# A two-layer DeltaNet and attention network on one core: an output head moved ahead of the recurrence's last round, a bank of its own for the last 256 columns, and four decayed values of the first step on GpSimd

## The chip, the core and the metric

The kernel runs as one program on one core of a Trainium2 chip. The core has a matrix engine (TensorE, PE in the profile; PEld is its weight load), a vector engine (VectorE, DVE), a scalar engine (ScalarE, ACT), a general engine (GpSimd, POOL) and a sync engine (SyncE, SP) that here only issues DMA transfers. Each engine works through its own list of instructions in order and waits at an instruction until the semaphores that it names are set. Matrix results go to PSUM, whose space is handed out in banks; everything else on the chip lies in SBUF, and the large intermediate arrays go out to the chip's memory (HBM) and come back.

The metric is the device time of one execution in microseconds (us), as the median of several runs. A profiled execution has its own time beside it; its span, from the first to the last record of the trace, is a little shorter.

## What is computed

The network has 512 latent tokens and 256 context tokens of width 1024 and two layers. Each layer is a modulated normalisation, a mixer, a gate and a residual sum. The mixer of layer 0 is a gated DeltaNet that runs over the tokens in both directions, with 16 value heads of 128 and chunks of 64 tokens; that of layer 1 is attention with 8 query heads, 2 key heads and an axial rotation. A last normalisation gives the output. What the change touches are the recurrence of layer 0, the output projection behind it and the end of the last layer:

```python
def step(s, xs):                                   # one chunk of 64 tokens, one direction
    qk_i, qd_i, kd_i, u_i, w_i, gl_i = xs
    v_new = u_i - jnp.einsum('bhcd,bhde->bhce', w_i, s)
    o = jnp.einsum('bhcd,bhde->bhce', qd_i, s) + jnp.einsum('bhcs,bhse->bhce', qk_i, v_new)
    s = s * gl_i[..., None, None] + jnp.einsum('bhcd,bhce->bhde', kd_i, v_new)
    return s, o
...
def finish(o, z):
    o = rms_norm(jnp.transpose(o, (0, 2, 1, 3)), o_norm_g).astype(z.dtype)
    return (o.reshape(b, l, DN_VAL_DIM) * jax.nn.silu(z)) @ w_out
...
        h_lat = h_lat + gate[:, None] * y_lat          # in both layers
...
    return rms_norm(h_lat, final_norm_g)
```

The state `s` starts at zero with the context, and what the context leaves in it is the start of the latent tokens.

## The kernel before, in words

**The recurrence.** It runs as 12 steps of one chunk in each direction (steps 0 to 3 the context, 4 to 11 the latent tokens), each in four parts of four heads. A piece is numbered x = 4·step + part, so there are 48. The loop `for x in range(50)` works on three pieces at a time: `products(x)`, `solve(x-1)`, `update(x-2)`.

- `products(x)` multiplies the state by keys and queries on PE (`ks`, L1562), forms the right side `r` on DVE (L1565), scales the query part into the output `O` or into `o` on ACT (L1568), and multiplies the state by its decay on POOL (`S`, L1571). On the second visit of a chunk POOL adds `o` into `O` (L1574). In step 0 the state is zero: there are no products, and `solve` takes the values directly.
- `solve(x)` multiplies by the inverted triangular matrices on PE (L1588) into the first half of a pair of PSUM banks, `pr_all` for even x and `pq_all` for odd x; ACT copies the result to `vn` (L1590); then four multiplications by a decay per token give `vd` (L1600 on ACT; in step 0, parts 0 and 1, L1598 on DVE).
- `update(x)` multiplies by the masked query-key products on PE (L1614) into the second half of the same pair of banks, and `vd` by the keys into `su` (L1622). The output is then copied (step 0, ACT, L1626) or added into `O` (DVE, L1628), and the state is copied (step 0, L1634) or added (L1636) on DVE.

As the banks alternate, `solve(x)` can only start when the reader of `update(x-2)`, at L1626 or L1628, is done with the same banks. There is one `su`, two each of `ks`, `r`, `vn` and `vd`.

**The order of the work.** PE, DVE, ACT and POOL follow the order in which this part of the program is written. SP's transfers are placed by the scheduler.

**The output seam.** The output projection of layer 0 runs over 32 units: two groups of three token tiles, 16 heads each. For one unit `out_load` (L1656) and `gate_load` (L1665) fetch the weights and the gate z; `out_high` (L1673, ACT) and `out_low` (L1680, POOL) split the weights into two parts `woh` and `wol`; `out_scale` (L1692, ACT) normalises the head's output into `so`; `out_turn` (L1699, PE) transposes it into `pt`; `out_gated` (L1708, DVE, three products) multiplies by the gate; `out_cast` (L1715, ACT) and `out_rest` (L1721, DVE) split the result into `y0` and `y1`; and `out_product` (L1742, PE) multiplies. The first unit's steps are written into the last rounds of the recurrence: the scaling at x = 45 and 46, the transposes at 46, gate, cast and rest at 47, between `solve(46)` and `update(45)`, and the first product at 48.

**The end.** In the last layer the output projection goes tile by tile (four of 128 tokens). `out_chunk` (L2442) runs the 24 matmuls of one chunk of columns, `finish_part` (L2448 to L2450) applies the gate, adds the residual and squares; `finish_sum` (L2454, L2456) and `finish_norm` (L2462 to L2465) give the inverse root, `weighed` (L2508) multiplies by the final weights. The last tile has three chunks, `(0, 512), (512, 256), (768, 256)`; the last two lie in the two halves of one bank, `po`. Behind the last one, ACT scales the first 512 columns (L2525) and DVE the others (L2527), and `send` (L2471) stores each half of the columns from the queue of ACT and of SP. A tile is made of 64 tokens each from two ends of the sequence, so `send` stores two pieces of 64 rows.

Of the kernel before, what the change touches and what calls it, by code (L numbers as in the profile page):

```python
# [12 lines left out]
ALU = mybir.AluOpType  # L13
# [4 lines left out]
P = 128  # L18
# [68 lines left out]
def backbone(tc, a, out):  # L87
# [1416 lines left out]
    if True:  # L1504
# [72 lines left out]
        def solve(x):  # L1577

            s, p = divmod(x, 4)
            t, visit = where(s)  # L1580
            Tt = loads[s][3]
            r, = live[x]
            pr_ = prq[x % 2][:, :, 0:2]
            for i in range(2):
                for j in range(2):
                    for hf in range(2):
                        r0, o0 = hf * 64, (hf ^ j) * 64
                        T.matmul(pr_[o0:o0 + 64, j, i], Tt[r0:r0 + 64, 4 * p + 2 * j + i, :], r[r0:r0 + 64, 2 * j + i], start=True, stop=True)  # L1588
            vn = ch.tile([P, 4, P], F32, tag="vn", name=f"vn{x}", bufs=2)
            (V.tensor_copy if x == 0 else S.copy)(vn.rearrange("p (j i) d -> p j i d", j=2), pr_)  # L1590
            vd = None
            if s < 11:
                vd = ch.tile([P, 4, P], F32, tag="vd", name=f"vd{x}", bufs=2)
                for c in range(4):
                    h = 4 * p + c
                    el = (elX if c > 1 else elV)[:, visit, t, h:h + 1]
                    if s == 0 and p < 2:
                        V.tensor_scalar(vd[:, c], vn[:, c], el, None, ALU.mult)  # L1598
                    else:
                        S.activation(vd[:, c], vn[:, c], AF.Copy, scale=el)  # L1600
            live[x] = [vn, vd]
# [99 lines left out]
    def out_gated(n, js=ALL):  # L1701

        gi, h = units0[n]
        pt, z = turned[n], zs_[n]
        for j in js:
            t, off, st_ = GROUPS[gi][j]
            pj = pt[:, j].rearrange("p (a k) -> p a k", a=2)
            V.scalar_tensor_tensor(pj, pj, og, raw(z, off, [[st_, 2], [1, 64]]), ALU.mult, ALU.mult)  # L1708
# [44 lines left out]
    AB, C = (0, 1), (2,)  # L1753
    squares = [(t, h) for t in (1, 0, 5) for h in range(VH)]
    for x in range(50):
        if x < 48:
            products(x)
        if x == 45:
            out_scale(0, AB)
        if x == 46:  # L1760
            out_scale(0, C)
        if 0 <= x - 1 < 48:
            solve(x - 1)
        if x == 47:
            out_gated(0)
            out_cast(0)
            out_rest(0)
        if 0 <= x - 2 < 48:
            update(x - 2)
        if x == 45:  # L1770
            psU_c.__exit__(None, None, None)
            psV_c = tc.tile_pool(name="psV", bufs=2, space=PSUM, reuse_waits="tile")
            turning["p"] = psV_c.__enter__()
        if 14 <= x < 30 or x >= 35:
            for t, h in squares[:2]:
                square_o(t, h)
            del squares[:2]
        if x == 1:
            V.tensor_tensor(or2, rq, rq, ALU.mult)
        if 30 <= x < 42:  # L1780
            some(ctx_chain, (2, 4, 1, 1, 1, 1, 1, 1, 1, 1, 1, 99)[x - 30])
        if x in (43, 44, 45):
            some(chain, (3, 7, 99)[x - 43])
        if x in (28, 32, 36, 40):
            with tc.issue_after(mark[0]):
                (out_load if x < 36 else gate_load)((x - 28) // 4 % 2)
        if x in (44, 45):
            out_high(x - 44)
        if x == 46:
            out_low(0)  # L1790
            out_turn(0)
        if x == 47:
            out_low(1)
            out_load(2)
        if x == 48:
            out_scale(1)
            out_product(0, 0)
            out_turn(1)
# [632 lines left out]
    gated(15)  # L2431


    acc = [pg, acc1, [tr_tile(f"pso2{nh}").rearrange("p a b -> p (a b)") for nh in range(2)], [s_all[:, 1024:1536], po]]

    jks = [f2.tile([P, D], F32, tag="jko", name=f"jko{t}") for t in range(2)]
    CHUNKS = [((0, 512), (512, 512))] * 3 + [((0, 512), (512, 256), (768, 256))]

    def out_chunk(k, t, c0, n):
        cc_, (bank, b0) = slice(c0, c0 + n), divmod(c0, 512)  # L2440
        for x, (i, j) in enumerate(PASS):
            T.matmul(acc[t][bank][:, b0:b0 + n], yT[i][:, k, t * P:(t + 1) * P], wo[j][:, k, cc_], start=k == 0 and x == 0, stop=k == KT - 1 and x == 2)  # L2442

    def finish_part(t, i):
        c0, n = CHUNKS[t][i]
        c, (bank, b0) = slice(c0, c0 + n), divmod(c0, 512)
        jk = jks[t]
        V.tensor_tensor(jk[:, c], acc[t][bank][:, b0:b0 + n], gate1[:, 0, c], ALU.mult)  # L2448
        V.tensor_tensor(hs[t][:, c], hs[t][:, c], jk[:, c], ALU.add)
        S.activation(jk[:, c], hs[t][:, c], AF.Square, accum_out=ss[:, t, i:i + 1])  # L2450
# [15 lines left out]
        return y  # L2466

    def send(t, x, c, q):
        for hf in range(2):
            c_ = t if hf == 0 else 7 - t  # L2470
            q(out[0, c_ * 64:c_ * 64 + 64, c], x[hf * 64:hf * 64 + 64, c])  # L2471
# [99 lines left out]
```

## Time and profile before

| | us |
|---|---|
| median of 3 runs | 1148.21 (1148.09 to 1150.12) |
| profiled execution, its own time | 1148.87 |
| its span | 1147.0 |
| PE busy | 1108.2 (97%) |
| DVE busy | 787.8 (69%) |
| ACT busy | 749.1 (65%) |
| POOL busy | 600.9 (52%) |
| granted PE clock (mean) | 0.995 |

The stages on the span's clock: the recurrence's first pieces start near 538, its step 1 near 548; from there to 709 it runs on; the seam lies between 709 and 718; the output projection fills the time to about 835; the last tile's matmuls end at 1136.2 and the last store is issued near 1142.8.

In the lines of the profile, L1588 is line 1588 of the kernel, `pr_all<-r,cT` names the tile written and those read, `128x512 f32` is partitions by elements, and `x16` the number of instructions in the row. In a timeline the first two numbers are start and duration in us, and the brackets hold the engine's idle time ahead of the row and what ended it. A row with several instructions gives the time from the first start to the last end. Matmuls are pipelined, so that consecutive rows of PE overlap a little.

### The profile page before, as it was taken

What the parts mean: (1) busy time and instruction counts of PE and PEld (TensorE: products, weight loads), DVE (VectorE), ACT (ScalarE), POOL (GpSimd) and SP (SyncE); (2) the same over time, 40 slices, a digit from 0 to 9 for tenths busy, and PEclk for the clock granted to TensorE, in tenths of its full rate; (3) what the DMA queues carried; (4) which work ended last, traced back from release to release, by engine and by line L of the source; (5) the groups of instructions that cost most, each with busy time, mean ns of one, the idle gap of its engine ahead of it and who ended that gap; (6) DMA issues with size and microseconds to landing.
All of it is one profiled execution on the core that took longest, in us unless ns stands there. A gap on an engine that the chain in (4) does not pass through costs nothing.

```text
span 1147.0 us, 27235 instructions
## 1 busy us (share of the span) xinstructions
PE 1108.2 (97%) x10511; PEld 904.6 (79%) x10511; DVE 787.8 (69%) x1628; ACT 749.1 (65%) x1998; POOL 600.9 (52%) x521
## 2 busy tenths in 40 slices
PE   5999999999999999998999999999999999999996
PEld 2777788888888888887566665888787889999885
DVE  4786656688899978783688877355546476667646
ACT  4554554477877888675789888875767356666731
POOL 0554111239999999940675688556645253130900
PEclk9999999999999999999999999999999999999999
DMA  9589744765748886756998983686844112001323
GB/s 367 199 287 326 261 143 130 226 178 166 232 128 241 264 246 205 207 181 193 291 258 244 276 252 101 196 224 184 239 136 138 55 57 63 30 19 56 111 74 92
DMA packets 117138, 208.69 MB, mean 182 GB/s; under 512 B 12145, under 2 KB 76818, under 8 KB 111762
## 3 DMA queue, kind: packets, MB, share of 16 engines
q1 hardware_dynamic: 97074, 195.32, 55.2%
q10 hardware_dynamic: 19936, 11.64, 3.4%
q8 instruction: 83, 1.36, 0.5%
q14 instruction: 45, 0.37, 0.1%
HBM read 166.16 MB, written 40.67 MB: 180 GB/s over the span
## 4 chain that ended last, share of the span: by engine, by line
PE 89%; DVE 3%; issue 2%; DMA 2%; ACT 2%; POOL 1%; SPq 0%; POOLq 0%; ACTq 0%; DVEq 0%
PE g_v L926 12%; PE g_z L926 12%; PE po L1742 9%; PE ks L1562 7%; PE g_k L500 6%; PE g_q L926 6%; PE pg L2162 4%; PE su L1622 3%; PE pg L2213 3%; PE po L2282 3%; PE s L2233 3%; PE kv L2044 2%; PE pa L316 2%; PE pt L2261 2%; PE pq_all L1588 1%
## 5 line engine op out<-in xcount | busy, mean ns | idle before, releaser
L1742 PE MATMUL po<-woh,y 128*128 128x512 f32 x384 | 129.2, 401 | 0.0
L1571 POOL TENSOR_TENSOR S<-S,glb 128x512 f32<-128x512 f32 x80 | 81.9, 1045 | 82.3 <-PE ks L1562 82.1
L1680 POOL TENSOR_TENSOR wol<-wo,woh 128x1024 fp32r<-128x1024 f32 x32 | 77.5, 2422 | 55.9 <-ACT woh L1673 54.2
L810 POOL TENSOR_TENSOR X<-X,tmp 128x62 f32<-128x62 f32 (+15 forms) x93 | 98.6, 1060 | 7.3
L809 POOL TENSOR_TENSOR tmp<-L,X 128x62 f32<-128x62 f32 (+15 forms) x93 | 91.9, 989 | 6.7
L926 PE MATMUL g_z<-uh,wh_z 128*128 128x512 f32 (+1 forms) x256 | 88.6, 346 | 0.0
L926 PE MATMUL g_v<-uh,wh_v 128*128 128x512 f32 (+1 forms) x256 | 88.0, 344 | 0.0
L941 DVE SCALAR_TENSOR_TENSOR acc_v<-g_v,cwv,acc_v 128x510 f32<-128x510 f32 (+3 forms) x128 | 77.7, 614 | 14.5 <-ACT acc_v L933 11.0
L926 PE MATMUL g_z<-ul,wh_z 128*128 128x512 f32 (+1 forms) x256 | 86.9, 339 | 0.4 <-issue 0.4
L926 PE MATMUL g_z<-uh,wl_z 128*128 128x512 f32 (+1 forms) x256 | 86.6, 338 | 0.0
L926 PE MATMUL g_v<-ul,wh_v 128*128 128x512 f32 (+1 forms) x256 | 86.1, 336 | 0.0
L926 PE MATMUL g_v<-uh,wl_v 128*128 128x512 f32 (+1 forms) x256 | 86.1, 336 | 0.0
L1742 PEld LDWEIGHTS po<-woh,y 128*128 128x128 f32 x384 | 72.3, 188 | 15.4 <-issue 0.3
L1742 PE MATMUL po<-wol,y 128*128 128x512 f32 x192 | 75.4, 393 | 0.0
L1636 DVE TENSOR_TENSOR S<-su,S 128x512 f32<-128x512 f32 x80 | 51.5, 686 | 8.1 <-PE su L1622 6.5
L1708 DVE SCALAR_TENSOR_TENSOR pt<-pt,og,z 128x128 f32<-128x128 f32 x96 | 34.4, 358 | 32.5 <-PE pt L1699 30.2
L555 POOL TENSOR_TENSOR kt<-kt,kss 128x768 f32<-128x768 f32 x8 | 11.6, 1472 | 85.6 <-DVE kss L183 57.1
L1562 PE MATMUL ks<-S,ck 128*64 128x256 f32 x352 | 55.4, 392 | 1.0 <-ACT O L1568 1.0
L1565 DVE SCALAR_TENSOR_TENSOR r<-ks,negV,cv 128x128 f32<-128x128 f32 x176 | 52.3, 344 | 5.2 <-PE ks L1562 2.2
L1562 PE MATMUL ks<-S,cq 128*64 128x256 f32 x352 | 53.6, 379 | 0.0
L926 PEld LDWEIGHTS g_z<-ul,wh_z 128*128 128x128 f32 x256 | 49.0, 191 | 5.4 <-issue 0.6
L926 PEld LDWEIGHTS g_z<-uh,wl_z 128*128 128x128 f32 x256 | 48.9, 191 | 5.4
(463 smaller groups left out, 3341.6 us busy)
## 6 DMA issues: line engine op xcount, KB each, us to landing
aw<-in_ada_late SPq DMA_DIRECT2D x16, 1024.0 KB, 7.3
wo<-in_dn_w_out SPq DMA_DIRECT2D x32, 512.0 KB, 3.7
cv<-v_d SPq DMA_DIRECT2D x22, 512.0 KB, 8.7
aw<-in_ada_first SPq DMA_DIRECT2D x8, 1024.0 KB, 11.6
w_z<-in_dn_w_in SPq DMA_DIRECT2D x16, 512.0 KB, 5.0
w_v<-in_dn_w_in SPq DMA_DIRECT2D x16, 512.0 KB, 4.5
v_d<-vt ACTq DMA_DIRECT2D x16, 384.0 KB, 4.2
cT<-t_d SPq DMA_DIRECT2D x12, 512.0 KB, 9.4
```

What stands on the lines that cost most here:

```text
L500: T.matmul(kbank[h, i][:, :n], w[:, k], u[:, k, c0:c0 + n], start=k == 0 and n_ == 0, stop=k == KT - 1 and n_ == len(passes) - 1)
L809: G.tensor_tensor(tv, bcast(L[:, :, j + 1:, j], 3, j + 1), bcast(X[:, :, j, 0:j + 1], 2, n), ALU.mult)
L810: G.tensor_tensor(X[:, :, j + 1:, 0:j + 1], X[:, :, j + 1:, 0:j + 1], tv, ALU.subtract)
L926: T.matmul(ps[:, :m], w[:, k], u[:, k, c0:c0 + m], start=k == 0 and n_ == 0, stop=k == KT - 1 and n_ == 2)
L941: V.scalar_tensor_tensor(acc[:, c0 + lo:c0 + hi], ps[:, lo + j - 2:hi + j - 2], cwv[:, j, ct:ct + 1], acc[:, c0 + lo:c0 + hi], ALU.mult, A ...
L1562: T.matmul(ks[r0:r0 + 64, w], kq[w][:, hh, r0:r0 + 64], St[hh][:, d], start=True, stop=True)
L1565: V.scalar_tensor_tensor(r[:, 2 * j + i], ks[:, 0, i], negV[:, visit, t, h:h + 1], v[:, h], ALU.mult, ALU.add)
L1571: G.tensor_tensor(St[hh], St[hh], bcast(g_, 3, P), ALU.mult)
L1636: V.tensor_tensor(St[hh], sj, St[hh], ALU.add)
L1680: G.tensor_tensor(wl, raws.pop(n), halves[n][0], ALU.subtract)
L1742: T.matmul(acc[nh], y[i][:, j, :], ww[k][:, nh * 512:(nh + 1) * 512], start=h == 0 and x == 0, stop=h == VH - 1 and x == 2)
L2162: T.matmul(q_bank(p, t), uL[i][:, k, t * P:(t + 1) * P], wq[j][:, k], start=k == 0 and n_ == 0, stop=k == KT - 1 and n_ == 2)
```

## The change

There are three parts.

1. In step 0 the four multiplications that make `vd` of parts 2 and 3 go from ACT to POOL, as two products over two heads each, with the decays read with a stride of zero.
2. In round x = 47 the first head's gate and cast come ahead of `products(47)`, and its rest comes behind `update(45)`.
3. The last tile's columns 768 to 1023 get the bank `pg[0]`, which the first tile used, in place of the second half of `po`; and the last tile, whose 64-row pieces (rows 192 to 255 and 256 to 319) lie side by side in the output, is stored by one transfer of 128 rows per queue instead of two of 64.

```diff
--- before.py
+++ after.py
@@ -1594,7 +1594,10 @@
                 for c in range(4):
                     h = 4 * p + c
                     el = (elX if c > 1 else elV)[:, visit, t, h:h + 1]
-                    if s == 0 and p < 2:
+                    if s == 0 and p > 1:
+                        if c % 2 == 0:
+                            G.tensor_tensor(vd[:, c:c + 2], vn[:, c:c + 2], bcast((elX if c > 1 else elV)[:, visit, t, h:h + 2], 2, P), ALU.mult)
+                    elif s == 0:
                         V.tensor_scalar(vd[:, c], vn[:, c], el, None, ALU.mult)
                     else:
                         S.activation(vd[:, c], vn[:, c], AF.Copy, scale=el)
@@ -1753,6 +1756,9 @@
     AB, C = (0, 1), (2,)
     squares = [(t, h) for t in (1, 0, 5) for h in range(VH)]
     for x in range(50):
+        if x == 47:
+            out_gated(0)
+            out_cast(0)
         if x < 48:
             products(x)
         if x == 45:
@@ -1761,12 +1767,10 @@
             out_scale(0, C)
         if 0 <= x - 1 < 48:
             solve(x - 1)
-        if x == 47:
-            out_gated(0)
-            out_cast(0)
-            out_rest(0)
         if 0 <= x - 2 < 48:
             update(x - 2)
+        if x == 47:
+            out_rest(0)
         if x == 45:
             psU_c.__exit__(None, None, None)
             psV_c = tc.tile_pool(name="psV", bufs=2, space=PSUM, reuse_waits="tile")
@@ -2431,19 +2435,22 @@
     gated(15)
 
 
-    acc = [pg, acc1, [tr_tile(f"pso2{nh}").rearrange("p a b -> p (a b)") for nh in range(2)], [s_all[:, 1024:1536], po]]
+    acc = [pg, acc1, [tr_tile(f"pso2{nh}").rearrange("p a b -> p (a b)") for nh in range(2)], [s_all[:, 1024:1536], po, pg[0]]]
 
     jks = [f2.tile([P, D], F32, tag="jko", name=f"jko{t}") for t in range(2)]
     CHUNKS = [((0, 512), (512, 512))] * 3 + [((0, 512), (512, 256), (768, 256))]
 
+    def place(t, c0):
+        return (2, 0) if t == 3 and c0 == 768 else divmod(c0, 512)
+
     def out_chunk(k, t, c0, n):
-        cc_, (bank, b0) = slice(c0, c0 + n), divmod(c0, 512)
+        cc_, (bank, b0) = slice(c0, c0 + n), place(t, c0)
         for x, (i, j) in enumerate(PASS):
             T.matmul(acc[t][bank][:, b0:b0 + n], yT[i][:, k, t * P:(t + 1) * P], wo[j][:, k, cc_], start=k == 0 and x == 0, stop=k == KT - 1 and x == 2)
 
     def finish_part(t, i):
         c0, n = CHUNKS[t][i]
-        c, (bank, b0) = slice(c0, c0 + n), divmod(c0, 512)
+        c, (bank, b0) = slice(c0, c0 + n), place(t, c0)
         jk = jks[t]
         V.tensor_tensor(jk[:, c], acc[t][bank][:, b0:b0 + n], gate1[:, 0, c], ALU.mult)
         V.tensor_tensor(hs[t][:, c], hs[t][:, c], jk[:, c], ALU.add)
@@ -2466,6 +2473,9 @@
         return y
 
     def send(t, x, c, q):
+        if t == 3:
+            q(out[0, 192:320, c], x[:, c])
+            return
         for hf in range(2):
             c_ = t if hf == 0 else 7 - t
             q(out[0, c_ * 64:c_ * 64 + 64, c], x[hf * 64:hf * 64 + 64, c])
```

The change's lines stand 3 to 10 below those of before from here on: L1628 becomes L1631, L1708 becomes L1711, L1721 becomes L1724.

Two places show how the instructions stand. The first is DVE's list at the end of the recurrence: `r46`, `r47` are the right sides of pieces 46 and 47, `pt0` the first head's transposed output, `O2` the output of token tile 2. Before:

```order
L1565 SCALAR_TENSOR_TENSOR r46_9670<-ks46_0_9672,negV_88,cv_11_9526 128x128 x2
L1565 SCALAR_TENSOR_TENSOR r46_9670<-ks46_1_9681,negV_88,cv_11_9526 128x128 x2
L1628 TENSOR_TENSOR O2_6912<-pr_all_6943,O2_6912 128x512
L1565 SCALAR_TENSOR_TENSOR r47_9717<-ks47_0_9719,negV_88,cv_11_9526 128x128 x2
L1565 SCALAR_TENSOR_TENSOR r47_9717<-ks47_1_9728,negV_88,cv_11_9526 128x128 x2
L1708 SCALAR_TENSOR_TENSOR pt0_9713<-pt0_9713,og_74,z0_0_9079 128x128 x3
L1721 TENSOR_TENSOR y1_0_0_9752<-pt0_9713,y0_0_0_9751 128x384
L1628 TENSOR_TENSOR O2_6912<-pq_all_6944,O2_6912 128x512
```

With the change:

```order
L1565 SCALAR_TENSOR_TENSOR r46_9666<-ks46_0_9668,negV_88,cv_11_9522 128x128 x2
L1565 SCALAR_TENSOR_TENSOR r46_9666<-ks46_1_9677,negV_88,cv_11_9522 128x128 x2
L1631 TENSOR_TENSOR O2_6912<-pr_all_6943,O2_6912 128x512
L1711 SCALAR_TENSOR_TENSOR pt0_9709<-pt0_9709,og_74,z0_0_9075 128x128 x3
L1565 SCALAR_TENSOR_TENSOR r47_9719<-ks47_0_9721,negV_88,cv_11_9522 128x128 x2
L1565 SCALAR_TENSOR_TENSOR r47_9719<-ks47_1_9730,negV_88,cv_11_9522 128x128 x2
L1631 TENSOR_TENSOR O2_6912<-pq_all_6944,O2_6912 128x512
L1724 TENSOR_TENSOR y1_0_0_9717<-pt0_9709,y0_0_0_9716 128x384
```

The three gated products now stand ahead of the two pairs for `r47`, and the addition out of `pq_all`, which frees the banks for `solve(47)`, stands ahead of the rest `y1` instead of behind it.

The second is ACT's list where step 0 passes into step 1 (`vd2` and `vd3` are the decayed values of parts 2 and 3, `O0` the output of token tile 0, `ks4` the products of piece 4). Before:

```order
L1590 COPY vn2_7010<-pr_all_6943 128x512
L1600 ACTIVATE vd2_7012<-vn2_7010,elV_89 128x128 x2
L1600 ACTIVATE vd2_7012<-vn2_7010,elX_90 128x128 x2
L1626 COPY O0_6910<-pq_all_6944 128x512
L1568 ACTIVATE O1_6911<-ks4_0_7051,egV_87 128x128 x2
L1568 ACTIVATE O1_6911<-ks4_1_7061,egV_87 128x128 x2
L1590 COPY vn3_7079<-pq_all_6944 128x512
L1600 ACTIVATE vd3_7081<-vn3_7079,elV_89 128x128 x2
L1600 ACTIVATE vd3_7081<-vn3_7079,elX_90 128x128 x2
L1626 COPY O0_6910<-pr_all_6943 128x512
L1568 ACTIVATE O1_6911<-ks5_0_7107,egV_87 128x128 x2
```

With the change:

```order
L1590 COPY vn2_7010<-pr_all_6943 128x512
L1629 COPY O0_6910<-pq_all_6944 128x512
L1568 ACTIVATE O1_6911<-ks4_0_7049,egV_87 128x128 x2
L1568 ACTIVATE O1_6911<-ks4_1_7059,egV_87 128x128 x2
L1590 COPY vn3_7077<-pq_all_6944 128x512
L1629 COPY O0_6910<-pr_all_6943 128x512
L1568 ACTIVATE O1_6911<-ks5_0_7103,egV_87 128x128 x2
```

ACT's copies out of `pq_all` and `pr_all` into `O0` now follow the copies `vn2` and `vn3` directly. The products went to POOL, whose list now reads as follows (`S0` and `S1` are the state's decays of piece 4; those of piece 5, `S2` and `S3`, come next):

```order
L1599 TENSOR_TENSOR vd2_7012<-vn2_7010,elV_89 128x256
L1599 TENSOR_TENSOR vd2_7012<-vn2_7010,elX_90 128x256
L1571 TENSOR_TENSOR S0_6935<-S0_6935,glb_91 128x512
L1571 TENSOR_TENSOR S1_6936<-S1_6936,glb_91 128x512
L1599 TENSOR_TENSOR vd3_7079<-vn3_7077,elV_89 128x256
L1599 TENSOR_TENSOR vd3_7079<-vn3_7077,elX_90 128x256
```

Before, the four decays stood there alone, one behind the other.

## The prediction

> **What bounds the kernel now.** I read the page first: shares by engine, then the chain that ended last; after that the idle time before TensorE's (PE) instructions, three timelines where the diff acts, and the windows between them.
>
> ```profile
> PE 1108.2 (97%) x10511; PEld 904.6 (79%) x10511; DVE 787.8 (69%) x1628; ACT 749.1 (65%) x1998; POOL 600.9 (52%) x521
> PE 89%; DVE 3%; issue 2%; DMA 2%; ACT 2%; POOL 1%; SPq 0%; POOLq 0%; ACTq 0%; DVEq 0%
> ```
>
> PE is busy for 97% of the span. An edit that adds or removes no matmul can therefore gain only where PE stands still, or behind its last matmul. Of PE's waits these four matter here (wait, releaser: total us, times, longest):
>
> ```profile
> PE pq_all L1588 <- DVE O L1628: 2.4, 1, 2.4
> PE pp L837 <- issue: 2.1, 1, 2.1
> PE su L1622 <- issue: 1.4, 1, 1.4
> PE pr_all L1588 <- ACT O L1626: 0.8, 1, 0.8
> ```
>
> The first and the last belong to the seam and to the first step of the recurrence, the two places that the diff reorders. The two "issue" waits have no releaser in the profile; they come back as a rival.
>
> **First step.** Around the 0.8 us wait (start, duration, engine, line; in brackets the idle time ahead):
>
> ```profile
> 546.93 1.12 DVE L1565 SCALAR_TENSOR_TENSOR r<-ks,negV,cv 128x128 f32<-128x128 f32 x4 [1.99 <-DMA cv<-v_d]
> 548.66 0.59 ACT L1590 COPY vn<-pq_all 128x512 f32<-128x512 f32 x1
> 549.28 0.69 ACT L1600 ACTIVATE vd<-vn,elV 128x128 f32<-128x128 f32 x2
> 549.48 2.04 POOL L1571 TENSOR_TENSOR S<-S,glb 128x512 f32<-128x512 f32 x2 [2.70 <-PE ks L1562]
> 549.65 0.60 PE L1562 MATMUL ks<-S,cq 128*64 128x256 f32 x4
> 550.46 0.57 ACT L1626 COPY O<-pr_all 128x512 f32<-128x512 f32 x1
> 551.08 0.67 PE L1588 MATMUL pr_all<-r,cT 64*64 64x128 f32 x16 [0.83 <-ACT O L1626]
> 552.01 1.04 PE L1622 MATMUL su<-vd,ckt 64*64 64x256 f32 x16
> ```
>
> The chain reads: part 3's copy to vn3, four ScalarE (ACT) multiplications for vd3 (two a row of 0.69 from 549.28, the others up to 550.46), then the copy of part 2's output out of the bank pr_all; part 4's solve overwrites that bank and waits. What stands before vn3 is set by a DMA (cv, at 546.93) and doesn't move. After the change the four multiplications leave ACT, so the copy starts when vn3 is done, 549.28, and ends near 549.85. PE is through with its own ks products at 549.65 + 0.60 = 550.25. The solve then goes at 550.25 instead of 551.08: **0.83 us**, the whole wait, with 0.4 us of cover left.
>
> What pays for it is GpSimd (POOL): two products of 128x256 for vd3, 549.3 onwards. The trace has no such operation on these tiles. The nearest row is of the same shape and engine:
>
> ```profile
> L358 POOL TENSOR_TENSOR y<-y,au 128x256 f32<-128x256 f32 x8 | 6.2, 772 | 13.7 <-ACT uh L352 13.7
> ```
>
> At 0.77 each vd3 is there at 550.1 (first half) and 550.9 (second). The state product su reads it at 552.01 − 0.83 = 551.18, its second half some 0.5 later, so up to about 0.95 per product costs nothing. From below, half of the 128x512 decay's 1.02 (2.04 for two) is 0.51; from above, 1.02, as if half the width cost the same. At 1.02 the second half would be ready at 551.4, against 551.7: still hidden. I take 0.77. Queued behind vd3 on POOL are the decays of S2 and S3 (549.48): they slip to about 550.9, end near 552.9, and are next needed by the addition into S2 behind part 5's su, which itself comes behind part 5's solve (554.86 before, 554.03 after): over 1 us of cover. The other pair, vd2, is freer still:
>
> ```profile
> 542.10 0.69 ACT L1600 ACTIVATE vd<-vn,elV 128x128 f32<-128x128 f32 x2
> 546.31 1.04 PE L1622 MATMUL su<-vd,ckt 64*64 64x256 f32 x16
> 554.86 0.67 PE L1588 MATMUL pq_all<-r,cT 64*64 64x128 f32 x16
> ```
>
> vn2 stands by 542.10, when its first multiplication begins now, and su reads vd2 at 546.31; two products of 0.77 from 542.10 on end at 543.7.
>
> Next late would be part 5's solve, at 554.03 after the shift, whose bank part 3's output copy on ACT must leave first. ACT has work without a gap there; I leave 0.4 for a slip. Term 0.83, bounds 0.4 and 0.83.
>
> **Seam.** The step of 2.4 us, in the timeline:
>
> ```profile
> 709.34 0.62 PE L1614 MATMUL pr_all<-vn,cQK 64*64 64x128 f32 x16
> 710.12 0.69 DVE L1628 TENSOR_TENSOR O<-pr_all,O 128x512 f32<-128x512 f32 x1 [0.54 <-PE pr_all L1614]
> 710.64 0.33 PE L1699 MATMUL pt<-ident,so 128*128 128x128 f32 x1 [0.32 <-ACT so L1692]
> 712.03 0.61 DVE L1565 SCALAR_TENSOR_TENSOR r<-ks,negV,cv 128x128 f32<-128x128 f32 x2 [1.22 <-PE ks L1562]
> 712.76 0.63 ACT L1568 ACTIVATE o<-ks,egV 128x128 f32<-128x128 f32 x2 [1.69 <-DVE r L1565]
> 713.26 0.62 PE L1614 MATMUL pq_all<-vn,cQK 64*64 64x128 f32 x16
> 713.42 1.14 DVE L1708 SCALAR_TENSOR_TENSOR pt<-pt,og,z 128x128 f32<-128x128 f32 x3
> 714.12 0.59 ACT L1590 COPY vn<-pr_all 128x512 f32<-128x512 f32 x1
> 714.59 0.49 ACT L1715 CAST y<-pt 128x384 fp32r<-128x384 f32 x1
> 715.11 0.56 DVE L1721 TENSOR_TENSOR y<-pt,y 128x384 fp32r<-128x384 f32 x1 [0.55 <-ACT y L1715]
> 715.59 0.68 DVE L1628 TENSOR_TENSOR O<-pq_all,O 128x512 f32<-128x512 f32 x1
> 716.32 0.67 PE L1588 MATMUL pq_all<-r,cT 64*64 64x128 f32 x16 [2.44 <-DVE O L1628]
> ```
>
> PE wrote its part of pq_all by 713.26 + 0.62 = 713.88. VectorE (DVE) could have added it into O then, and freed the bank for part 47's solve. In its queue stand the head's three gated products, a wait of 0.55 for ACT's cast, and the rest y1, so the addition starts at 715.59. After the change the gated products run as soon as the head's last transpose is done, 710.64 + 0.33 = 710.97, in DVE's idle 1.22 us: to about 712.16. Part 47's first pair of r (712.03) is 0.15 late, and even two pairs of 0.61 in a row end by 713.4, ahead of 713.88. The addition then starts at 713.88 plus the 0.16 that lie between PE's end at 709.34 + 0.62 and the addition before it (710.12): 714.04. It ends at 714.72, and the solve goes at 714.77 instead of 716.32: **1.55 us**. The cast on ACT takes 712.25 to 712.74 and ends as part 47's first o is due (712.76), so vn46 at 714.12 stays. The rest y1 comes behind the addition, 714.72 to 715.28, and the first to read it is the first output product, which on PE comes behind part 47's solve and part 46's update, both over 0.5: near 715.8. If the gated products waited for something that I don't see until 712.03, the cast would push vn46 some 0.8 back and PE lose 0.3: lower bound 1.2. On SyncE's queue the head's z loads come ahead of the next weight load; both gate on buffers that come free early, so I cost that at nothing.
>
> Does PE keep what these two give?
>
> ```profile
> 551.00:677.00 126.00, 125.88 (x2124) 81.59 (x2128) 100.74 (x230) 109.53 (x376) 86.80 (x91) 1.00 0.93 263
> 677.00:681.00 4.00, 2.65 (x48) 1.56 (x42) 1.40 (x4) 3.43 (x13) 2.52 (x4) 1.00 0.80 300
> 720.00:815.00 95.00, 95.00 (x444) 77.43 (x445) 47.02 (x108) 68.04 (x210) 57.60 (x27) 1.00 0.70 208
> ```
>
> Columns: length, then PE, weight load, DVE, ACT, POOL, clock, DMA share, GB/s. Behind the first step PE is busy 125.88 of 126.00 us, behind the seam 95.00 of 95.00. It waits for nobody, so an earlier start is an earlier end. Against it stands the DMA share of 0.93: the recurrence's loads run near what the queues move. That is rival C.
>
> **Tail.** The last tile's end, with the stores and their landing times:
>
> ```profile
> 1130.39 5.83 PE L2442 MATMUL po<-wo,yT 128*128 128x256 f32 x48
> 1136.26 0.42 DVE L2448 TENSOR_TENSOR jko<-po,gate 128x256 f32<-128x256 f32 x1 [2.39 <-PE po L2442]
> 1137.85 0.41 DVE L2448 TENSOR_TENSOR jko<-po,gate 128x256 f32<-128x256 f32 x1
> 1142.25 1.20 ACTq L2471 DMA_DIRECT2D out<-hg  x2
> out<-jko SPq DMA_DIRECT2D x6, 256.0 KB, 3.3
> hs<-h_d SPq DMA_DIRECT2D x1, 512.0 KB, 4.0
> out<-hg ACTq DMA_DIRECT2D x2, 128.0 KB, 2.7
> ```
>
> The 48 matmuls are two chunks of 24 into one bank. The first chunk is complete near 1133.3, half-way, yet DVE, idle for 2.39 and so free from 1133.87, waits until 1136.26, when the bank's last matmul is done. With a bank of its own for the second chunk, the first chunk's work (1137.85 − 1136.26 = 1.59 us up to the next multiplication) runs from 1133.9 to 1135.5 under PE, with 0.75 of cover. The second multiplication starts at 1136.26, and all behind it is 1.59 earlier. The store on ACT's queue: before, two issues of 0.60, the second at 1142.85, landing at 1145.55 by 2.7. After, one of 256 KB at 1140.66, landing at 1143.96 by the row of 256 KB. What the single issue saves (0.60), the larger transfer costs (3.3 − 2.7). **1.59 us**; 2.2 if it landed in 2.7, 0.9 if it took the 4.0 of the 512 KB row. DVE's half on SyncE's queue, at 1140.33, lands before it.
>
> By the Trainium skill, page "DMA: Bandwidth & Descriptors", section "Anatomy of one DMA — SWDGE (gpsimd) path", a transfer takes a fixed 2.0 us or so and its bytes over 436e3 per us. As an estimate from that page, doubling 128 KB adds 0.3, the tail would give 1.9, and the sum below would end at 1143.9. The trace's 0.6 between the two rows speaks against so small a step, and I go by the rows.
>
> **Sum.** 0.83 + 1.55 + 1.59 = 3.97 us. The profiled execution took 1148.87, so 1144.90; it lay 0.66 above the median of 1148.21, so the forecast for the median is **1144.2 us**. No term depends on another.
>
> **Rivals.**
>
> B, *the first step's gain stays out*: POOL's vd3 comes later than su needs it, as its product slows beside DVE or waits in POOL's queue. From 0.95 per product on, each tenth costs 0.2, and at 1.4 the 0.83 is gone: 1145.0. For it: POOL now does ahead of PE what ACT did. Against it: POOL's rows are far from 1.4, 0.77 for this shape and 1.02 for twice the width, at this very place. Beside this the Trainium skill, "SBUF — State Buffer", section "SBUF: two separate sides", says that a DVE instruction with two SBUF inputs and a GpSimd one exclude each other for their whole length. DVE's r reads ks from PSUM and only cv from SBUF, so by that rule it blocks nothing; the trace has no such pair to compare. Chance 0.15.
>
> C, *only the tail's gain stays*: the transfers set the pace of the recurrence (DMA share 0.93), so PE waits later for what it gained. 1148.21 − 1.59 = 1146.6. Against it: PE idles 0.12 in 126 us, so no load was late there; for it: how early they were isn't in that row. Chance 0.18.
>
> D, *slower*: a stall of the "issue" kind. Two stand in the list, 2.1 and 1.4, one of them inside the recurrence's 677 to 681, where PE is busy 2.65 of 4.00 without a releaser. If they depend on how PE's stream meets the transfers, shifting PE by 0.83 and 1.55 can call up others. One costs at most 2.1 and leaves a gain of 1.9; two (4.2) cancel the 3.97, and from the third on the kernel is slower: 1148.21 − 3.97 + 6.3 = 1150.5. Against it: two in 10511 matmuls. Chance 0.06.
>
> **How the numbers follow.** Forecast 0.61, B 0.15, C 0.18, D 0.06. Best bounds: 0.83 + 1.55 + 2.2 = 4.6, 1143.6; the 0.66 between two executions of one kernel takes the low end to 1142.9. Above, the range reaches to C with 0.4: 1147.0. What three runs can tell from no change is 0.2%, 2.3 us: faster means under 1145.9. The forecast and B lie there (0.03 of them lost to a store or a stall); C doesn't. Faster 0.73, same 0.21, slower 0.06.
>
> **What would show it.** First step: the wait of pr_all for ACT's O gone, POOL's 128x256 products between 0.5 and 0.95, no wait of su for vd. Seam: the wait of pq_all for O at 0.9 instead of 2.4, the gated products ahead of r. Tail: DVE's multiplication of the first 256 columns before PE's last matmul, the second right behind it, one store of about 3.3. PE busy less than 125.8 of the 126 us behind the first step would speak for C, new issue waits for D. The forecast is wrong if the median is above 1145.9.

## The result, and the profile after

The changed kernel takes 1144.36 us (median of 22 runs, 1142.75 to 1149.89), the kernel before 1150.41 (median of 22, 1147.43 to 1155.74). The ratio is 0.9952, 95% interval 0.9939 to 0.9964: faster by 0.48%, or 5.5 us of 1150.4, between 4.1 and 7.0 (the two medians by themselves lie 6.05 apart). The forecast of 1144.2 stood on three runs of before with a median of 1148.21, and on a gain of 3.97. Its absolute time was hit; the gain was forecast a little smaller than the interval allows (3.97 against 4.1), and its three terms didn't come out as priced.

The profiled execution of the changed kernel took 1147.86, so it is one of its longer ones, as that of before (1148.87) was one of its shorter ones. The two spans differ by 0.9 us only, and a reader who subtracts them is misled. The page of the changed kernel:

```profile
span 1146.1 us, 27231 instructions
PE 1110.3 (97%) x10511; PEld 907.8 (79%) x10511; DVE 788.5 (69%) x1628; ACT 747.2 (65%) x1990; POOL 602.6 (53%) x525
```

The same matmuls in both traces show where the spans part (start in us):

| PE instruction | before | changed | later by |
|---|---|---|---|
| a z projection ahead of the recurrence, L926 | 530.38 | 533.24 | 2.86 |
| ks of piece 5 (step 1), L1562 | 548.31 | 550.12 | 1.81 |
| solve of piece 4, L1588 | 551.08 | 551.99 | 0.91 |
| ks of piece 9 (step 2), L1562 | 564.84 | 566.46 | 1.62 |
| update of piece 45, pq_all, L1614 and L1617 | 713.26 | 716.44 | 3.18 |
| solve of piece 47, L1588 | 716.32 | 717.97 | 1.65 |
| end of PE's last matmul | 1136.22 | 1137.84 | 1.62 |
| end of the trace | 1147.01 | 1146.08 | −0.93 |

2.86 us of lateness were there before the first instruction that the change touches. Between there and the solve of piece 4, 1.95 of it went, mostly because the trace of before has two waits that this one hasn't: 0.96 at the ks of piece 5, where ACT and DVE stood behind late values (L1565 behind cv, 1.99 in the prediction), and the 0.83 of the first step. The seam took 1.53 of it back (3.18 to 1.65), and PE kept that to its last matmul; the tail took 2.55 (from 1.62 later to 0.93 earlier). Between them PE lost time again, at places that the waits of PE name (the same view as before):

```profile
PE g_z L926 <- issue: 1.5, 2, 0.9
PE su L1625 <- issue: 1.4, 1, 1.4
PE pq_all L1617 <- issue: 1.3, 1, 1.3
PE ks L1562 <- ACT o L1568: 1.2, 1, 1.2
PE pq_all L1588 <- DVE O L1631: 0.9, 1, 0.9
```

The last row is the seam's wait, 2.4 before. The 0.8 of pr_all for ACT's O is not in the list. The other four weren't put there by the change: two of the "issue" rows have their like before (su 1.4, g_z 0.4), and the other two stand as well in the runs below whose recurrence is that of before: pq_all 1.3 and 1.2, ks 0.5 and 1.0 with the bank alone and the stores alone.

The seam's timeline after, to hold against the twelve rows in the prediction:

```profile
714.18 1.15 DVE L1711 SCALAR_TENSOR_TENSOR pt<-pt,og,z 128x128 f32<-128x128 f32 x3 [0.20 <-PE pt L1702]
715.24 0.60 DVE L1565 SCALAR_TENSOR_TENSOR r<-ks,negV,cv 128x128 f32<-128x128 f32 x2
715.69 0.48 ACT L1718 CAST y<-pt 128x384 fp32r<-128x384 f32 x1 [1.45 <-PE ks L1562]
716.44 0.62 PE L1617 MATMUL pq_all<-vn,cQK 64*64 64x128 f32 x16
717.22 0.69 DVE L1631 TENSOR_TENSOR O<-pq_all,O 128x512 f32<-128x512 f32 x1 [0.54 <-POOL wol L1683]
717.83 0.55 DVE L1724 TENSOR_TENSOR y<-pt,y 128x384 fp32r<-128x384 f32 x1
717.97 0.67 PE L1588 MATMUL pq_all<-r,cT 64*64 64x128 f32 x16 [0.91 <-DVE O L1631]
```

The gated products fill DVE's pause, and the addition follows PE's 716.44 + 0.62 = 717.06 by 0.16, as forecast. Its bracket names POOL, but PE's end lies nearer. The first step:

```profile
549.56 0.59 ACT L1590 COPY vn<-pq_all 128x512 f32<-128x512 f32 x1
550.02 0.61 ACT L1629 COPY O<-pr_all 128x512 f32<-128x512 f32 x1
550.22 0.61 POOL L1599 TENSOR_TENSOR vd<-vn,elV 128x256 f32<-128x256 f32 x1 [0.66 <-ACT vn L1590]
550.79 0.62 POOL L1599 TENSOR_TENSOR vd<-vn,elX 128x256 f32<-128x256 f32 x1
551.99 0.67 PE L1588 MATMUL pr_all<-r,cT 64*64 64x128 f32 x16
552.92 1.04 PE L1625 MATMUL su<-vd,ckt 64*64 64x256 f32 x16
565.07 1.13 DVE L1565 SCALAR_TENSOR_TENSOR r<-ks,negV,cv 128x128 f32<-128x128 f32 x4 [2.12 <-DMA cv<-v_d]
```

POOL's products take 0.61, not 0.77, and end 1.5 us ahead of su. But PE's solve had nothing to wait for: with four multiplications of the old length behind vn3 (550.15 + 1.28) the copy would have ended near 552.0, when PE was ready anyway. And 13 us behind the solve DVE waits 2.12 us for the values of step 2, which costs PE the 1.2 of the list. The tail:

```profile
1134.84 3.00 PE L2449 MATMUL pg<-wo,yT 128*128 128x256 f32 x24
1135.41 0.41 DVE L2455 TENSOR_TENSOR jko<-po,gate 128x256 f32<-128x256 f32 x1
1137.88 0.42 DVE L2455 TENSOR_TENSOR jko<-pg,gate 128x256 f32<-128x256 f32 x1 [0.81 <-PE pg L2449]
1142.28 0.34 ACTq L2477 DMA_DIRECT2D out<-hg  x1
out<-hg SPq DMA_DIRECT2D x1, 256.0 KB, 2.1
```

DVE's first 256 columns run under PE, the second follow its end (1137.84) at once, and SyncE's store of 256 KB lands in 2.1 us where 3.3 was forecast. The forecast was for ACT's store, whose landing this view doesn't have; with the stores alone it is 2.4.

### The profile page after: what moved, and what is told of

It is laid out like the page before. It is cut to its first block, busy times and chain, and to the rows that moved or that the text cites. A ratio compares the mean times of both kernels' runs of the same rounds, so it can differ in the third digit from the quotient of the medians.

```text
span 1146.1 us, 27231 instructions
## 1 busy us (share of the span) xinstructions
PE 1110.3 (97%) x10511; PEld 907.8 (79%) x10511; DVE 788.5 (69%) x1628; ACT 747.2 (65%) x1990; POOL 602.6 (53%) x525
## 5 line engine op out<-in xcount | busy, mean ns | idle before, releaser
L810 POOL TENSOR_TENSOR X<-X,tmp 128x62 f32<-128x62 f32 (+15 forms) x93 | 102.9, 1107 | 7.3
L809 POOL TENSOR_TENSOR tmp<-L,X 128x62 f32<-128x62 f32 (+15 forms) x93 | 88.4, 951 | 6.7
L926 PE MATMUL g_z<-uh,wh_z 128*128 128x512 f32 (+1 forms) x256 | 88.4, 345 | 0.9 <-issue 0.9
L926 PE MATMUL g_v<-uh,wh_v 128*128 128x512 f32 (+1 forms) x256 | 87.9, 344 | 0.0
L926 PE MATMUL g_z<-ul,wh_z 128*128 128x512 f32 (+1 forms) x256 | 86.9, 339 | 0.6 <-issue 0.6
L926 PE MATMUL g_z<-uh,wl_z 128*128 128x512 f32 (+1 forms) x256 | 86.8, 339 | 0.0
L926 PE MATMUL g_v<-ul,wh_v 128*128 128x512 f32 (+1 forms) x256 | 86.1, 336 | 0.0
L926 PE MATMUL g_v<-uh,wl_v 128*128 128x512 f32 (+1 forms) x256 | 86.1, 336 | 0.0
L1711 DVE SCALAR_TENSOR_TENSOR pt<-pt,og,z 128x128 f32<-128x128 f32 x96 | 34.3, 358 | 32.7 <-PE pt L1702 30.4
L1562 PE MATMUL ks<-S,ck 128*64 128x256 f32 x352 | 55.1, 392 | 1.2 <-ACT o L1568 1.2
L1565 DVE SCALAR_TENSOR_TENSOR r<-ks,negV,cv 128x128 f32<-128x128 f32 x176 | 52.3, 344 | 3.5 <-DMA cv<-v_d 2.1
L926 PEld LDWEIGHTS g_z<-ul,wh_z 128*128 128x128 f32 x256 | 48.9, 191 | 6.5 <-issue 1.8
L926 PEld LDWEIGHTS g_z<-uh,wh_z 128*128 128x128 f32 x256 | 48.9, 191 | 5.4
L926 PEld LDWEIGHTS g_z<-uh,wl_z 128*128 128x128 f32 x256 | 48.8, 191 | 5.3
```

What stands on the lines that cost most here:

```text
L809: G.tensor_tensor(tv, bcast(L[:, :, j + 1:, j], 3, j + 1), bcast(X[:, :, j, 0:j + 1], 2, n), ALU.mult)
L810: G.tensor_tensor(X[:, :, j + 1:, 0:j + 1], X[:, :, j + 1:, 0:j + 1], tv, ALU.subtract)
L926: T.matmul(ps[:, :m], w[:, k], u[:, k, c0:c0 + m], start=k == 0 and n_ == 0, stop=k == KT - 1 and n_ == 2)
L1562: T.matmul(ks[r0:r0 + 64, w], kq[w][:, hh, r0:r0 + 64], St[hh][:, d], start=True, stop=True)
L1565: V.scalar_tensor_tensor(r[:, 2 * j + i], ks[:, 0, i], negV[:, visit, t, h:h + 1], v[:, h], ALU.mult, ALU.add)
```

## The experiments

Theory after the result: the seam gives 1.5, the bank 1.6 and the stores 0.9, while the first part gives 0.8 only in executions in which the values of step 1 come late. Rivals: the first part does give its 0.8 in general (the prediction); the transfers take back what PE gains early (C).

**The parts alone.** All four against the same runs of before. The first part:

```diff
-                    if s == 0 and p < 2:
+                    if s == 0 and p > 1:
+                        if c % 2 == 0:
+                            G.tensor_tensor(vd[:, c:c + 2], vn[:, c:c + 2], ...)
+                    elif s == 0:
```

> Only the first part: the decayed values of parts 2 and 3 of step 0 on GpSimd. Theory (the prediction's): PE's wait of pr_all for ACT's O (0.8 before) is gone and nothing takes its place there; 0.83 us faster. Rival B (GpSimd late): the products take 0.95 us or more each, PE waits at the state product su for vd, and the gain is 0 to 0.3. Rival C (transfers set the pace): the wait is gone, but PE waits longer for a load (r behind cv) within the next two steps, and the gain is 0 to 0.3 in time.

Measured: ratio 0.9994 (0.9981 to 1.0006), that is −0.7 us between −2.2 and +0.7. The wait is gone, but the time alone can't tell 0.8 from nothing. The profiles of the kernels that lack this part tell more: the wait isn't there either. In the run with the bank alone:

```profile
547.86 0.69 ACT L1600 ACTIVATE vd<-vn,elV 128x128 f32<-128x128 f32 x2
549.05 0.56 ACT L1626 COPY O<-pr_all 128x512 f32<-128x512 f32 x1
549.66 0.67 PE L1588 MATMUL pr_all<-r,cT 64*64 64x128 f32 x16
```

The four multiplications stand on ACT as before, the copy ends at 549.61, and PE goes on at 549.66, 0.09 later than it could. Of six profiles without the first part and with the loads untouched, that of before has the 0.83; in the five others this wait for ACT is 0 to 0.1. In these five DVE waited at most 0.22 for the values of step 1, in that of before 1.99.

The second part, as in the change's diff for round 47:

> Only the second part: the first output head's gate and cast ahead of round 47, its rest behind the update. Theory: PE's wait of pq_all for DVE's O goes from 2.4 to 0.9 and everything behind starts 1.5 to 1.7 earlier; 1.5 to 1.7 us faster. Rival C: the wait shrinks as much, but a wait for a transfer grows behind it, and the time gains under 0.5.

Measured: ratio 0.9981 (0.9965 to 0.9997), −2.2 us between −4.0 and −0.3; the wait of pq_all fell to 0.9. At the solve of piece 47 PE was 2.81 earlier than before's (1.28 of it from earlier on, 1.53 from the seam), at its last matmul 2.62: the gain was kept. Early in the recurrence, this run shows rival C at work, in PE's waits and in DVE's row:

```profile
562.19 1.13 DVE L1565 SCALAR_TENSOR_TENSOR r<-ks,negV,cv 128x128 f32<-128x128 f32 x4 [2.73 <-DMA cv<-v_d]
563.57 0.65 PE L1562 MATMUL ks<-S,ck 128*64 128x256 f32 x4 [1.78 <-ACT o L1568]
```

PE had come up to this place early, 3.12 ahead of before at the su of L1622 just ahead of it, and gave back 1.85 at this wait for the values of step 2.

The traces show one thing more at the seam, for which the forecast has no term. With the bank alone the long wait is still there, and behind it PE's granted clock is halved for 3.4 us; the second row is the same stretch of the changed kernel (columns as in the prediction, the clock third from the end):

```profile
714.39 0.91 PE L1588 MATMUL pq_all<-r,cT 64*64 64x128 f32 x16 [2.44 <-DVE O L1628]
714.70:718.10 3.40, 3.40 (x37) 2.68 (x27) 0.69 (x1) 2.71 (x7) 1.46 (x2) 0.50 0.54 160
717.90:721.30 3.40, 3.33 (x54) 2.68 (x57) 1.17 (x3) 2.38 (x5) 3.20 (x2) 1.00 0.44 154
```

Of the eight profiles with the wait of 2.44, five have this stretch (the bank's, and the four below whose loads were moved), and PE lost 1.3 to 1.7 us in it against before; the other three, that of before among them, don't. Of the six with a shorter wait, 0.9 or 1.3, none has it. The timed runs fit: their mean granted clock is 0.9922 for before (33 runs), 0.9924, 0.9923 and 0.9922 for the first part, the bank and the stores alone, but 0.9938 for the seam alone and 0.9942 for the whole change. One stretch of 3.4 us at half the clock makes 0.0015 of 1147 us, so, as an estimate, the second part spares about one such stretch in an execution, some 1.5 us beside the 1.53 of the wait. Why the clock falls in some executions and not in others was not tested.

The bank alone:

```diff
-    acc = [..., [s_all[:, 1024:1536], po]]
+    acc = [..., [s_all[:, 1024:1536], po, pg[0]]]
...
+    def place(t, c0):
+        return (2, 0) if t == 3 and c0 == 768 else divmod(c0, 512)
```

> Only the bank of its own for the last 256 columns; the stores stay four of 64 rows. Theory: from PE's last matmul to the end of the trace 1.59 us less than before's 10.79, that is 9.2. If the bank were not what held DVE back, the wait of 2.39 would stay and so would 10.8.

Measured: ratio 0.9976 (0.9962 to 0.9991), −2.8 us between −4.4 and −1.0. PE's last matmul ends at 1135.97, the trace at 1145.22: 9.25, against 10.79, so 1.54 less. In the eight other profiles of these experiments whose end is that of before, this stretch is 10.5 to 11.05, so a difference between two single profiles is good to some 0.3.

The stores alone:

```diff
     def send(t, x, c, q):
+        if t == 3:
+            q(out[0, 192:320, c], x[:, c])
+            return
         for hf in range(2):
```

> Only the stores: one of 128 rows per queue instead of two of 64. The prediction's pricing by rows: the issue saved (0.60) is lost in a longer transfer (3.3 instead of 2.7), so PE's last matmul to the end stays at 10.8 and the time within 0.2. Against it, as the changed kernel's trace reads: the store of 128 rows lands in about 2.1, and the stretch falls to 9.8 to 9.9, 0.9 to 1.0 us faster.

Measured: ratio 0.9987 (0.9975 to 1.0000), −1.5 us between −2.9 and 0. PE's end to the trace's end: 9.97, so 0.82 less than before's. DVE's wait for the bank stands as it was; the stores are what changed:

```profile
1138.80 0.42 DVE L2448 TENSOR_TENSOR jko<-po,gate 128x256 f32<-128x256 f32 x1 [2.39 <-PE po L2442]
out<-hg ACTq DMA_DIRECT2D x1, 256.0 KB, 2.4
```

256 KB landed in 2.4, and before 128 KB in 2.7. The second expectation held, and the prediction's pricing fell. Bank and stores add up: 10.79 − 1.54 − 0.82 = 8.43, against 8.24 with both. The four times add up to 7.2, against 5.5 for the whole; with intervals of some 3 us each that is no contradiction.

**Why the merged store is cheaper.** In the changed kernel each last store goes out in two pieces again, by columns instead of by rows:

```diff
-            q(out[0, 192:320, c], x[:, c])
+            for c0 in (c.start, c.start + 256):
+                q(out[0, 192:320, c0:c0 + 256], x[:, c0:c0 + 256])
```

> The changed kernel with each of the two last stores in two pieces of 128 rows by 256 columns. If it was the number of transfers that made the stores dear, the stretch from PE's last matmul to the end goes back to the 9.2 of the run with the bank alone. If it was that 64 rows spread badly, it stays at 8.2 to 8.6.

```profile
1140.30 0.87 ACTq L2478 DMA_DIRECT2D out<-hg  x2
out<-hg ACTq DMA_DIRECT2D x2, 128.0 KB, 2.1
```

The stretch was 8.35 (one profile). So it is not the number of transfers, nor their bytes: 128 KB over 128 rows land in 2.1, over 64 rows in 2.7. The issue is shorter too: two of them take 0.87 here, two of 64 rows 1.20, the merged store 0.34. The Trainium skill, page "DMA: Bandwidth & Descriptors", section "Rules for kernel authors", says not to split a transfer into two halves of the partitions, since both go through the same engines, and to use one of 128 partitions. The runs agree with the advice, but its reason would hold for two pieces by columns as well, and these cost next to nothing more (8.35 against 8.24). Why 64 rows are slower was not measured; their rows in the output are also twice as long as those of the column pieces.

**What makes the first step's wait.** If the 0.83 came with late values, making them late must bring it back. First the values of step 1 were loaded a second time, in the kernel before and in the kernel with the first part:

```diff
         dma(Tt, t_d[t, :, visit])
         dma(QK, qk_d[t, :, visit])
+        if again is not None:
+            values_loaded(t, again)
...
-            mark[0] = matrices_loaded(t, visit, Tt, QK, kt)
+            mark[0] = matrices_loaded(t, visit, Tt, QK, kt, v if s == 1 else None)
```

> The kernel before, with the values of step 1 loaded a second time behind the first, so that they surely come late. Theory now: the wait of 0.8 of PE's pr_all for ACT's O belongs to executions in which these values are late; ACT's vn3 then stands behind the late o, and vd3 and the copy follow it. Here the wait is 0.7 to 0.9, though it was 0 to 0.1 in the three profiles without the first part and with the values in time. If the wait hangs on something else, it is 0 to 0.2 here too.

> The same late values with the first part of the change (vd of parts 2 and 3 on GpSimd). Theory now: the wait of pr_all for ACT's O is 0 to 0.1, the products are hidden, and the first part is worth 0.8 in this state alone. Rival B: PE waits at su for vd instead, by 0.3 or more.

Neither decided anything. The values came 15 us late, and PE then ran at half its clock, as the window of 562 to 566 of the first shows (columns as in the prediction):

```profile
562.92 1.12 PE L1564 MATMUL ks<-S,ck 128*64 128x256 f32 x4 [15.31 <-ACT O L1570]
562.00:566.00 4.00, 3.08 (x16) 1.72 (x16) 2.47 (x7) 3.71 (x12) 1.01 (x1) 0.50 0.97 215
```

At a granted clock of 0.50 PE's own ks products lasted until after the copy of O (565.64), and no wait could appear with or without the first part. The Trainium skill, page "TensorE: Matmul & The Clock Gate", section "What's actually happening", puts the idle clock at half rate, which agrees with this row. So a milder delay: the values behind the matrix T in the same queue.

```diff
         dma(Tt, t_d[t, :, visit])
+        if behind is not None:
+            values_loaded(t, behind)
         dma(QK, qk_d[t, :, visit])
...
-            values_loaded(t, v)
-            mark[0] = matrices_loaded(t, visit, Tt, QK, kt)
+            if s != 1:
+                values_loaded(t, v)
+            mark[0] = matrices_loaded(t, visit, Tt, QK, kt, v if s == 1 else None)
```

> The kernel before, with the values of step 1 loaded behind the matrix T of that step instead of ahead of it, so that they come some 2 us later and PE's pause stays short enough for its clock to hold (in the run that loaded them twice PE paused 15 us and then ran at a clock of 0.50, which hid the wait). Theory now: PE's wait of pr_all for ACT's O is 0.7 to 0.9, as in the profile before, because the late values put ACT's vn3, vd3 and the copy behind each other. If it hangs on something else, it is 0 to 0.2.

```profile
547.97 1.13 DVE L1568 SCALAR_TENSOR_TENSOR r<-ks,negV,cv 128x128 f32<-128x128 f32 x4 [2.88 <-DMA cv<-v_d]
550.32 0.69 ACT L1603 ACTIVATE vd<-vn,elV 128x128 f32<-128x128 f32 x2
551.51 0.56 ACT L1629 COPY O<-pr_all 128x512 f32<-128x512 f32 x1
552.12 0.67 PE L1591 MATMUL pr_all<-r,cT 64*64 64x128 f32 x16 [0.82 <-ACT O L1629]
```

DVE waited 2.88 for the values (1.99 in the profile before), and the wait of 0.82 was there again. With the five profiles above, where DVE waited at most 0.22 and PE at most 0.1, this ties it to late values.

> The same order of loads with the first part of the change. Theory now: the wait of pr_all for ACT's O is 0 to 0.1, PE's solve follows its own products, and su doesn't wait for GpSimd's vd. Rival B: a wait of 0.3 or more at su.

The wait was absent, but this execution doesn't decide: an issue wait of 0.80 ahead of the step made PE late itself, its mean granted clock was 0.59 over 544 to 548.2, and DVE waited for the values only 0.75.

```profile
544.00:548.20 4.20, 4.18 (x26) 1.91 (x26) 1.90 (x4) 0.62 (x2) 1.04 (x1) 0.59 0.87 357
550.74 0.61 POOL L1602 TENSOR_TENSOR vd<-vn,elX 128x256 f32<-128x256 f32 x1
551.94 0.67 PE L1591 MATMUL pr_all<-r,cT 64*64 64x128 f32 x16
```

That GpSimd's products are hidden it does show, as in every profile with this part. That they save the 0.8 when the values are late stays an argument from the order on ACT.

**Which half of the seam counts.** Only the gate and the cast ahead of round 47, the rest left between `solve(46)` and `update(45)`:

```diff
+        if x == 47:
+            out_gated(0)
+            out_cast(0)
         if x < 48:
             products(x)
...
         if x == 47:
-            out_gated(0)
-            out_cast(0)
             out_rest(0)
```

And the other half alone: gate and cast stay where they were, and only `out_rest(0)` goes behind `update(45)`.

> Of the second part only the gate and the cast ahead of round 47; the rest stays ahead of the update's addition. By the prediction's times the rest then ends about when PE is done with pq_all (714.06 against 714.04), so the wait of pq_all for O falls from 2.4 to 0.9 or 1.0, as with the whole part. If the place of the rest is what matters, it stays at 1.5 or more.

> Of the second part only the rest behind the update; gate and cast stay behind r of part 47. The addition then starts when the gated products end (714.56 in the prediction's times), 1.03 earlier than before: the wait of pq_all for O falls from 2.4 to 1.4. If the place of the gate doesn't matter, it falls to 0.9.

```profile
713.90 0.55 DVE L1721 TENSOR_TENSOR y<-pt,y 128x384 fp32r<-128x384 f32 x1
714.50 0.69 DVE L1628 TENSOR_TENSOR O<-pq_all,O 128x512 f32<-128x512 f32 x1
715.25 0.67 PE L1588 MATMUL pq_all<-r,cT 64*64 64x128 f32 x16 [0.89 <-DVE O L1628]
```

```profile
713.40 1.14 DVE L1708 SCALAR_TENSOR_TENSOR pt<-pt,og,z 128x128 f32<-128x128 f32 x3
714.44 0.68 DVE L1628 TENSOR_TENSOR O<-pq_all,O 128x512 f32<-128x512 f32 x1
715.18 0.67 PE L1588 MATMUL pq_all<-r,cT 64*64 64x128 f32 x16 [1.32 <-DVE O L1628]
```

The gate alone (first fence) brings the wait to 0.89, as the whole part does; the rest alone (second) to 1.32. With the gate moved, the place of the rest is worth nothing measurable (one profile each).

**A narrower last chunk.** On the changed kernel, 384 and 128 columns in place of 256 and 256:

```diff
-    CHUNKS = [((0, 512), (512, 512))] * 3 + [((0, 512), (512, 256), (768, 256))]
+    CHUNKS = [((0, 512), (512, 512))] * 3 + [((0, 512), (512, 384), (896, 128))]
```

> The changed kernel with the last tile's second and third chunk of 384 and 128 columns instead of 256 and 256. Behind PE's last matmul two DVE instructions and one of ACT work on half the columns: some 0.13 each from the rows of 0.42, so the stretch to the end falls from 8.2 to about 7.85. If PE's matmul of 128 columns takes half of that of 256 (0.125), this is 0.35 us faster than the changed kernel; if it takes as long, PE ends 1.5 later and the whole is 1.1 slower.

```profile
1126.36 4.33 PE L2449 MATMUL po<-wo,yT 128*128 128x384 f32 x24
1130.52 2.79 PE L2449 MATMUL pg<-wo,yT 128*128 128x128 f32 x24
1133.35 0.29 DVE L2455 TENSOR_TENSOR jko<-pg,gate 128x128 f32<-128x128 f32 x1 [0.57 <-PE pg L2449]
```

Behind PE's end the stretch fell to 7.86 as expected. But the 24 matmuls of 128 columns take 2.79, almost the 3.00 of 256, so the two chunks last 6.95 (1126.36 to 1133.31) instead of 5.83. That is 0.7 slower on balance, and the time (0.9967 of before, 0.9951 to 0.9983) shows no gain over the changed kernel's 0.9952. Of the kernels timed more than once, the change as it stands has the lowest ratio.

## Why the prediction was right or wrong

**The seam (1.55): right.** The wait fell by 1.53, from 2.44 to 0.91, by the mechanism named: the gated products in DVE's pause, the addition 0.16 behind PE, the rest harmless behind it. PE kept the gain, as the windows of continuous work behind the seam had said. What the forecast had at nothing, without a word, is the clock: the wait of 2.44 was followed by 3.4 us at a granted clock of 0.50 in five profiles of eight, and the shorter one in none of six. The profile before, on which the forecast stood, is one of the three without it.

**The tail (1.59): the mechanism right, the store mis-sized.** The bank gave 1.54 alone. The store's term was put at nothing, and it gave 0.82 alone and about 1.0 together with the bank: the whole tail 2.55, beyond the 2.2 that I had as its best. The step that failed is the choice of the row: "out<-jko, 256.0 KB, 3.3" has the bytes of the merged store but not its shape. It belongs to two stores of 64 rows by 1024 columns that follow each other in one queue; the merged store has 128 rows by 512. By bytes the price should have risen, by rows it fell. The issue saved (0.60) was priced rightly; the landing was to rise by 0.6 and fell, from 2.7 to 2.4 on ACT's queue. The fit of the Trainium skill that I weighed there (page "DMA: Bandwidth & Descriptors", section "Anatomy of one DMA — SWDGE (gpsimd) path"), a fixed part plus bytes, is given for transfers that GpSimd issues, and these go out from ACT and SyncE; it erred in the same way, with a rise of 0.3. The advice on partition halves, on the same page, is what bore on it.

**The first step (0.83): wrong as a gain of the median.** The step that failed is "what stands before vn3 is set by a DMA and doesn't move": I took the lateness of that one execution for a property of the kernel. With the values in time, ACT's copy comes as PE needs it, and there is nothing to remove. The row that carried the warning was quoted, with its 1.99 us of waiting for cv. GpSimd's part was as forecast: hidden (0.61 per product, bounds 0.51 to 1.02), and rival B did not come about. Its price was not consistent: 0.95 per product was its start, but by the prediction's own count a second half at 1.02 was still in time, and by that count the start lies near 1.2.

**Rival C** was right for this stage and wrong for the kernel. PE waited behind the values of step 2 in seven of the fourteen profiles, for 0.15 to 1.78 us, and for 1.17 in the changed kernel; in the six of them that have the landing on record, DVE's r starts 0.12 behind it. A gain at step 1 is worth something only when these values are in time too. But what was gained at the seam, behind the recurrence, was kept.

**Rival D** didn't come about, in that the change added no such waits, but they are not spread at random. One of 0.5 to 1.8 us falls on the same matmul, the pq_all of piece 9's update (578.31 in the changed kernel), in all nine profiles in which DVE waited 0.5 or less for the values of step 1, and in none of the five in which it waited 0.75 or more. Most of the others, 0.6 to 1.7, fall on su of piece 32 or 36. With the bank alone and the stores alone, whose recurrence is that of before, PE had gained 1.80 and 1.87 on before between the g_z row of the table and the solve of piece 4, since the values of step 1 came in time there; behind the waits at step 2 and at piece 9, at 577, it had 0.05 of the first left, and of the second nothing. So 0.83 saved at the first step need not reach the kernel's end even where it is there to be saved. What sets these waits off the runs don't show.

**The sum.** 1.53 + 2.55, and 0 to 0.8 for the first step, make 4.1 to 4.9; with the clock behind the seam, some 1.5 by the estimate above, 5.6 without the first step, against 5.5 (4.1 to 7.0) measured. The interval is too wide to tell these apart. The 3.97 came near by luck: 0.83 that was mostly not there stood in for 0.96 at the stores and what the clock gave, both left out. That the absolute forecast met the median within 0.2 us owes something to a second chance: the three runs of before were 2.2 below the median of 22, and its profile, with a mean granted clock of 0.995, had no stretch at half clock at the seam.

## What to carry to other kernels

A wait in one profiled execution is a property of the kernel only if what precedes it is: where a DMA wait stands just ahead, ask whether the wait is still there when that load is in time, before pricing its removal. A wait of PE can cost more than its length: look at the granted clock of the stretch behind it, in more than one profile. Price a transfer by a row of its own shape (rows by bytes per row, and what precedes it in its queue), not of its size. And two kernels of this noise are compared by the same instruction in both traces, place by place; their spans say little.

## What the runs showed of the hardware that was not expected

- A store of 128 rows lands sooner than one of half the bytes over 64 rows: on ACT's queue 2.4 for 128 by 512, 2.1 for 128 by 256, 2.7 to 2.8 for 64 by 512; on SyncE's 2.1, 1.9 and 2.2 to 2.9 (f32, last stores of the kernel, both queues busy; the smaller ones two behind each other).
- After 15.3 us of rest PE's granted clock was 0.50 over 562 to 566, with four ks products in 1.12 instead of 0.65. Much shorter rests can do it too: 2.44 us at the seam in five of eight profiles, and an issue wait of 1.66 with the stores alone (0.50 over 667.1 to 670.5); a rest of 1.78 with the seam alone did not (1.00 over 562 to 567).
- 24 matmuls of 128 columns in this weight order take 2.79 us, of 256 columns 3.00, of 384 columns 4.33: below 256 columns there is next to nothing to win.
- GpSimd's product with a broadcast factor took 0.61 for 128x256, where the TENSOR_TENSOR row of the same shape in another stage (y<-y,au) has 0.77.
